# Row scaling of the softmax weights in the latent attention: GpSimd alone, or two blocks each on GpSimd and ScalarE

## Chip, cores and metric

The kernel runs on one core of one Trainium2 chip. The metric is the device time of one execution in microseconds (us), taken as the median of several runs. For the kernel before it is 1179.66 us (three runs, 1179.07 to 1180.35).

The core has five engines that run side by side, each taking its own instructions strictly in order: TensorE (PE in the profile; its weight loads are PEld), VectorE (DVE), ScalarE (ACT), GpSimd (POOL) and SyncE (SP, which here only starts transfers). They wait for each other by semaphores.

## Reference

Two layers of an encoder on 512 tokens of 1024 channels, float32. Each layer normalises its input, projects it by one wide matrix, runs three token mixers side by side, gates and merges them, and adds the projected sum to the stream. The part at stake is the first mixer, the latent attention (MLA), with 8 heads:

```python
def attend(qb):                       # one block of 128 query rows, all heads
    s = jnp.einsum('bqhd,bkhd->bhqk', qb, k).astype(jnp.float32) * scale
    p = jax.nn.softmax(s, axis=-1).astype(v.dtype)
    return jnp.einsum('bhqk,bkhd->bqhd', p, v)
```

So for each head there is a 512 x 512 matrix P = exp(s - rowmax), of which each row is divided by its sum before it is multiplied by V. The other two mixers are a windowed attention with sinks and a differential attention; they have softmaxes of their own that the change does not touch.

## The kernel before, in words

Matrix products are done in a split form: each float32 operand is cut into a high part (a rounded copy, written by ScalarE with `act_copy`, line 81) and a low part (the rest, by VectorE with `sub`, line 84), and `mm3` (lines 86 to 89) adds the three products high x high, high x low and low x high. A projection of 128 columns (`proj_T`) is therefore 24 matmuls into the PSUM tile `ps_dn`. Its weights come through `wunit` (lines 102 to 116): a 512 KB load into `wr` (two buffers), a ScalarE cast to `wh` (three buffers), a VectorE subtraction to `wl` (three buffers). The `wr` buffers are also used by `mod_late` (line 245), which loads the next layer's modulation weights during layer 0 and multiplies them up on VectorE (line 251).

Latent attention (`mla_attention`) goes head by head in a software pipeline (`pipelined`): `first(h+1)` is issued ahead of `second(h)`.

- `first(h)`: for each of four blocks of 128 query rows, scores into `ps_sc` (`mm3`), the negated row maximum on VectorE (line 770), the exponential on ScalarE with the row sums as by-product (line 771), all into one tile `p` of 128 x 4 x 512 (two buffers). Then one VectorE reciprocal of the four columns of sums (line 773), and four scalings of 128 x 512 in place (line 775), one for each block, all on GpSimd.
- `second(h)`: for each of four blocks of keys, the four 128 x 128 pieces of P are transposed by TensorE into `ps_tr` (line 704), split into high and low `pt` (ScalarE line 81, VectorE line 84), and multiplied by V into `ps_av` (lines 711 to 717). Every one of these transposes' groups reads all four row blocks of P.

The order on each engine is not written by hand. The program is a list in program order; a planner takes instructions off it by priority (`tc.high_priority` moves weight units ahead) and by the times that it reckons for each operation and engine, and fixes each engine's queue from that. Projections that come later in the program (the gates of `gates_early`, the queries of the windowed attention) are so placed between the matmuls of the latent attention. Replacing one operation by another can thus change the queues behind it, beyond the operation itself.

Of the kernel before, what the change touches and what calls it, by code (L numbers as in the profile page):

```python
# [14 lines left out]
ALU = mybir.AluOpType  # L15
# [35 lines left out]
def hybrid_kernel(ctx, tc, x, c, w_ada, b_ada, g_pre, g_post, w_in, g_q, w_uq, g_kv, w_ukv,  # L51
# [6 lines left out]
    pe, act, dve, pool, sp = nc.tensor, nc.scalar, nc.vector, nc.gpsimd, nc.sync  # L58
# [4 lines left out]
    def T(tag, shape, dt=F32, bufs=None):  # L63
        count[0] += 1
        return sb.tile(shape, dt, tag=tag, name=f"{tag}_{count[0]}",
                       bufs=bufs or BUFS.get(tag, 1))

    def stat(n):
        return T("st", [P, n], F32, 24)
# [3 lines left out]
    def Q(tag):  # L73
        count[0] += 1
        return ps.tile([P, S], F32, tag=tag, name=f"ps_{tag}_{count[0]}", bufs=PB[tag])

    def f(ap):
        return ap.bitcast(F32)

    def act_copy(out_, in_, scale=1.0):  # L80
        return act.activation(out=out_, in_=in_, func=AF.Copy, scale=scale)  # L81

    def sub(out_, a, b, eng=None):
        return (eng or dve).tensor_tensor(out=out_, in0=a, in1=b, op=ALU.subtract)  # L84

    def mm3(o, ah, al, bh, bl, start, stop):
        pe.matmul(o, ah, bh, start=start, stop=False)  # L87
        pe.matmul(o, ah, bl, start=False, stop=False)  # L88
        pe.matmul(o, al, bh, start=False, stop=stop)  # L89
# [575 lines left out]
    def mla_pair_weights(l, p, tag="pt"):  # L665
        raw = T(tag, [P, S])
        qraw = raw[:, 0:384].rearrange("p (k c) -> p k c", k=2)
        kraw = T(tag, [P, S])[:, 0:256]
        with behind(loads[-2]) if l == 0 else nullcontext():
            sp.dma_start(out=qraw, in_=w_uq[l][:, p * 192:(p + 1) * 192]  # L670
                         .rearrange("(k p) c -> p k c", p=P))
            sp.dma_start(out=kraw, in_=w_ukv[l][:, p * 256:(p + 1) * 256])
        h = T("x5", [P, 2, 640], F32R)
        with behind():
            for k in range(2):
                src = raw[:, k * 192:(k + 1) * 192].rearrange("p (h c) -> p h c", h=2)
                hv = h[:, 0, k * 256:(k + 1) * 256].rearrange("p (h c) -> p h c", h=2)
                lv = h[:, 1, k * 256:(k + 1) * 256].rearrange("p (h c) -> p h c", h=2)
                g = par(l, PR_GQ, k)
                for dst, s0, n in ((0, 0, 96), (96, 80, 16), (112, 64, 16)):  # L680
                    act_copy(hv[:, :, dst:dst + n], src[:, :, s0:s0 + n], g)
                    dve.scalar_tensor_tensor(out=lv[:, :, dst:dst + n], in0=src[:, :, s0:s0 + n],
                                             scalar=g, in1=f(hv[:, :, dst:dst + n]),
                                             op0=ALU.mult, op1=ALU.subtract)
            src = kraw.rearrange("p (h c) -> p h c", h=2)[:, :, 0:64]
            hv = h[:, 0, 512:640].rearrange("p (h c) -> p h c", h=2)
            lv = h[:, 1, 512:640].rearrange("p (h c) -> p h c", h=2)
            g = par(l, PR_GKV)
            act_copy(hv, src, g)
            dve.scalar_tensor_tensor(out=lv, in0=src, scalar=g, in1=f(hv),  # L690
                                     op0=ALU.mult, op1=ALU.subtract)
        return h

    def pipelined(first, second, n):
        prev = first(0)
        for i in range(n):
            nxt = first(i + 1) if i + 1 < n else None
            second(i, prev)
            prev = nxt

    def transposed_block(blocks):
        tr = Q("tr")
        for i, b in enumerate(blocks):
            pe.transpose(tr[:, i * P:(i + 1) * P], b, ident)  # L704
        ph = T("pt", [P, S], F32R)
        pl = T("pt", [P, S], F32R)
        act_copy(ph, tr)
        sub(pl, tr, f(ph))
        return ph, pl

    def av_step(av, v, ph, pl, first, last):
        if not last:
            pe.matmul(av, v, ph, start=first, stop=False)  # L713
            pe.matmul(av[0:64], v[:, 0:64], pl, start=False, stop=False)  # L714
        else:
            pe.matmul(av[0:64], v[:, 0:64], pl, start=False, stop=False)
            pe.matmul(av, v, ph, start=False, stop=True)

    def mla_attention(l, cl, kp, v, wts):
        o_all = []  # L720
        ks, qs = {}, {}

        def weights(p):
            if p < 4 and p not in wts:
                wts[p] = mla_pair_weights(l, p)

        def prep(h):
            if h >= 8:
                return
            p, i = h // 2, h % 2  # L730
            w = wts[p]
            if i == 0:
                ts = [T("op", [P, S], F32R) for _ in range(4)]
                ka = Q("pj")
                mm3(ka, w[:, 0, 512:640], w[:, 1, 512:640], cl[2][:, 0], cl[2][:, 1], True, True)
                for j in range(2):
                    kh, kl = ts[2 * j:2 * j + 2]
                    src = ka[j * 64:(j + 1) * 64]
                    act_copy(kh[0:64], src)
                    sub(kl[0:64], src, f(kh[0:64]))  # L740
                    dve.tensor_copy(out=kh[64:128], in_=f(kp[0:64]))
                    dve.tensor_copy(out=kl[64:128], in_=f(kp[64:128]))
                    ks[h + j] = (kh, kl)
                weights(p + 1)
            qh = T("op", [P, S], F32R)
            ql = T("op", [P, S], F32R)
            qa = Q("pj")
            for k in range(2):
                lo = k * 256 + i * P
                mm3(qa, w[:, 0, lo:lo + P], w[:, 1, lo:lo + P], cl[k][:, 0], cl[k][:, 1],  # L750
                    k == 0, k == 1)
            qf = T("ta", [P, S])
            dve.tensor_tensor(out=qf, in0=qa, in1=rq, op=ALU.mult)
            act_copy(qh, qf)
            sub(ql, qf, f(qh))
            qs[h] = (qh, ql)

        def first(h):
            prep(h + 1)
            if h % 2 == 0:  # L760
                o_all.append(T("o", [P, S]))
            kh, kl = ks[h]
            qh, ql = qs[h]
            pr = T("p", [P, NT, S])
            nm, sm, rr = stat(NT), stat(NT), stat(NT)
            for t in range(NT):
                ts_ = slice(t * P, (t + 1) * P)
                s = Q("sc")
                mm3(s, qh[:, ts_], ql[:, ts_], kh, kl, True, True)
                dve.tensor_reduce(out=nm[:, t:t + 1], in_=s, axis=AX.X, op=ALU.max, negate=True)  # L770
                act.activation(out=pr[:, t], in_=s, func=AF.Exp, bias=nm[:, t:t + 1],  # L771
                               accum_out=sm[:, t:t + 1])
            dve.reciprocal(out=rr, in_=sm)  # L773
            for t in range(NT):
                pool.tensor_scalar(out=pr[:, t], in0=pr[:, t], scalar1=rr[:, t:t + 1],  # L775
                                   scalar2=1.0, op0=ALU.mult, op1=ALU.mult)
            return pr

        def second(h, pr):
            i = h % 2  # L780
            op = o_all[h // 2]
            av = Q("av")
            for kb in range(NT):
                ph, pl = transposed_block([pr[:, t, kb * P:(kb + 1) * P] for t in range(NT)])
                av_step(av, v[kb][:, h], ph, pl, kb == 0, kb == NT - 1)
            ol = T("ta", [P, S])
            act_copy(ol[0:64], av[64:128])
            dve.tensor_tensor(out=op[i * 64:(i + 1) * 64], in0=av[0:64], in1=ol[0:64], op=ALU.add)

        weights(0)  # L790
        prep(0)
        pipelined(first, second, 8)
        return o_all

# [425 lines left out]
```

## Time and profile before

| | |
|---|---|
| median of 3 runs | 1179.66 us (1179.07 to 1180.35) |
| the profiled execution | 1178.78 us, of which the span of the trace is 1176.7 us |
| mean granted TensorE clock | 0.993 |
| PE busy | 1146.0 us (97%) |
| DVE busy | 844.2 us (72%) |
| ACT busy | 631.5 us (54%) |
| POOL busy | 181.3 us (15%) |
| the 64 scalings of line 775, POOL | 52.2 us, 834 ns each on average |

The latent attention lies at about 117 to 260 us (layer 0) and 680 to 829 us (layer 1). "Busy" is the time in which an engine had an instruction in execution; TensorE's matmuls overlap, so two that follow each other without a gap start about 0.23 us apart though each is listed with 0.39 us. A row of a group gives count, busy time, mean duration of one, then the idle time of that engine just before these instructions and what ended it. A row of the timeline gives start, duration, engine, line, operation and tiles, and in brackets the idle time before it.

### The profile page before, as it was taken

What the parts mean: (1) busy time and instruction counts of PE and PEld (TensorE: products, weight loads), DVE (VectorE), ACT (ScalarE), POOL (GpSimd) and SP (SyncE); (2) the same over time, 40 slices, a digit from 0 to 9 for tenths busy, and PEclk for the clock granted to TensorE, in tenths of its full rate; (3) what the DMA queues carried; (4) which work ended last, traced back from release to release, by engine and by line L of the source; (5) the groups of instructions that cost most, each with busy time, mean ns of one, the idle gap of its engine ahead of it and who ended that gap; (6) DMA issues with size and microseconds to landing.
All of it is one profiled execution on the core that took longest, in us unless ns stands there. A gap on an engine that the chain in (4) does not pass through costs nothing.

```text
span 1176.7 us, 15536 instructions
## 1 busy us (share of the span) xinstructions
PE 1146.0 (97%) x5428; PEld 946.0 (80%) x5428; DVE 844.2 (72%) x1754; ACT 631.5 (54%) x1250; POOL 181.3 (15%) x226
## 2 busy tenths in 40 slices
PE   5899999999999999999999999999999999999997
PEld 4768788878887888888888888888888888888886
DVE  7956686898866687876577567688786568786654
ACT  5355464655543457664357456565564346675432
POOL 4310212122210010101211011222121001100120
PEclk9899999999999999999999999999999999999999
DMA  9537532256355433433454432324533333334442
GB/s 340 190 92 217 186 106 76 72 145 186 108 141 164 110 81 87 117 107 126 143 184 135 114 108 75 86 52 123 157 97 92 95 95 96 88 99 115 136 159 92
DMA packets 169522, 146.86 MB, mean 125 GB/s; under 512 B 7679, under 2 KB 146999, under 8 KB 169444
## 3 DMA queue, kind: packets, MB, share of 16 engines
q1 hardware_dynamic: 166148, 140.08, 40.9%
q10 hardware_dynamic: 3168, 5.77, 1.3%
q8 instruction: 43, 0.70, 0.2%
q14 instruction: 35, 0.29, 0.1%
q0 software_dynamic: 128, 0.01, 0.0%
HBM read 135.83 MB, written 14.20 MB: 127 GB/s over the span
## 4 chain that ended last, share of the span: by engine, by line
PE 84%; DVE 6%; DMA 3%; issue 3%; ACT 1%; POOL 1%; SPq 0%; DVEq 0%; POOLq 0%; ACTq 0%
PE ps_dn L87 20%; PE ps_dn L89 20%; PE ps_dn L88 19%; PE ps_tr L704 5%; PE ps_sc L89 2%; PE ps_sc L87 2%; PE ps_sc L88 2%; PE ps_av L714 1%; PE ps_av L713 1%; PE ps_sc L952 1%; PE ps_sc L953 1%; DMA wr<-in_w_in 1%; DVE o L206 1%; PE ps_pj L87 1%; PE ps_pj L88 1%
## 5 line engine op out<-in xcount | busy, mean ns | idle before, releaser
L87 PE MATMUL ps_dn<-hTh,wh 128*128 128x512 f32 x840 | 331.8, 395 | 1.4 <-DVE zz L479 0.8
L89 PE MATMUL ps_dn<-hTh,wl 128*128 128x512 f32 x840 | 330.5, 393 | 0.4 <-DVE wl L84 0.4
L88 PE MATMUL ps_dn<-hTl,wh 128*128 128x512 f32 x840 | 330.1, 393 | 0.0
L84 DVE TENSOR_TENSOR wl<-wr,wh 128x1024 fp32r<-128x1024 f32 x141 | 178.9, 1269 | 98.5 <-ACT wh L81 97.5
L81 ACT ACTIVATE wh<-wr 128x1024 fp32r<-128x1024 f32 x141 | 149.1, 1058 | 162.7 <-PE ps_dn L88 111.2
L87 PEld LDWEIGHTS ps_dn<-hTh,wh 128*128 128x128 f32 x840 | 158.2, 188 | 33.2 <-PE ps_dn L89 1.0
L89 PEld LDWEIGHTS ps_dn<-hTh,wl 128*128 128x128 f32 x840 | 158.0, 188 | 33.3 <-DVE wl L84 0.9
L88 PEld LDWEIGHTS ps_dn<-hTl,wh 128*128 128x128 f32 x840 | 158.1, 188 | 31.7
L84 DVE TENSOR_TENSOR pt<-ps_tr,pt 128x512 fp32r<-128x512 f32 x136 | 92.2, 684 | 30.5 <-ACT pt L81 29.6
L81 ACT ACTIVATE pt<-ps_tr 128x512 fp32r<-128x512 f32 x136 | 78.8, 596 | 64.8 <-PE ps_tr L704 63.6
L775 POOL TENSOR_SCALAR p<-p,st 128x512 f32<-128x512 f32 x64 | 52.2, 834 | 279.3 <-DVE st L773 243.7
L704 PE MATMUL ps_tr<-ident,p 128*128 128x128 f32 x544 | 92.4, 273 | 0.9 <-POOL p L775 0.6
L704 PEld LDWEIGHTS ps_tr<-ident,p 128*128 128x128 f32 x544 | 69.5, 141 | 20.2 <-POOL p L775 1.8
L87 PE MATMUL ps_dn<-u,wh 128*128 128x512 f32 x192 | 75.9, 395 | 0.0
L89 PE MATMUL ps_dn<-u,wl 128*128 128x512 f32 x192 | 75.9, 395 | 0.0
L88 PE MATMUL ps_dn<-u,wh 128*128 128x512 f32 x192 | 75.2, 391 | 0.0
L963 POOL TENSOR_SCALAR ta<-ta,st 128x512 f32<-128x512 f32 x32 | 26.7, 834 | 306.9 <-ACT wh L81 143.1
L894 POOL TENSOR_SCALAR p<-p,st 128x256 f32<-128x256 f32 (+1 forms) x64 | 42.1, 676 | 157.7 <-DVE st L892 130.4
L771 ACT ACTIVATE p<-ps_sc,st 128x512 f32<-128x512 f32 x64 | 43.7, 685 | 28.0 <-DVE st L770 27.7
L770 DVE TENSOR_REDUCE st<-ps_sc 128x1 f32<-128x512 f32 x64 | 43.4, 686 | 21.3 <-PE ps_sc L89 20.8
L886 ACT ACTIVATE p<-p,st 128x256 f32<-128x256 f32 (+1 forms) x64 | 35.7, 558 | 21.9 <-DVE st L884 21.2
L959 ACT ACTIVATE p<-p,st 128x512 f32<-128x512 f32 x32 | 23.1, 723 | 38.8 <-DVE st L957 38.7
(345 smaller groups left out, 2100.5 us busy)
## 6 DMA issues: line engine op xcount, KB each, us to landing
wr<-in_w_in SPq DMA_DIRECT2D x105, 512.0 KB, 3.7
wr<-in_w_ada SPq DMA_DIRECT2D x32, 512.0 KB, 3.6
wr<-in_w_out SPq DMA_DIRECT2D x16, 512.0 KB, 3.6
big<-in_w_ada SPq DMA_DIRECT2D x10, 512.0 KB, 7.6
big<-in_x SPq DMA_DIRECT2D x8, 512.0 KB, 5.3
wr<-in_w_o_mla SPq DMA_DIRECT2D x8, 512.0 KB, 4.0
wr<-in_w_o_swa SPq DMA_DIRECT2D x8, 512.0 KB, 3.4
wr<-in_w_o_diff SPq DMA_DIRECT2D x8, 512.0 KB, 3.7
```

The source lines that it names most:

```text
L81: return act.activation(out=out_, in_=in_, func=AF.Copy, scale=scale)
L84: return (eng or dve).tensor_tensor(out=out_, in0=a, in1=b, op=ALU.subtract)
L87: pe.matmul(o, ah, bh, start=start, stop=False)
L88: pe.matmul(o, ah, bl, start=False, stop=False)
L89: pe.matmul(o, al, bh, start=False, stop=stop)
L704: pe.transpose(tr[:, i * P:(i + 1) * P], b, ident)
L770: dve.tensor_reduce(out=nm[:, t:t + 1], in_=s, axis=AX.X, op=ALU.max, negate=True)
L771: act.activation(out=pr[:, t], in_=s, func=AF.Exp, bias=nm[:, t:t + 1], accum_out=sm[:, t:t + 1])
L775: pool.tensor_scalar(out=pr[:, t], in0=pr[:, t], scalar1=rr[:, t:t + 1], scalar2=1.0, op0=ALU.mult, op1=ALU.mult)
L886: act.activation(out=pr[:, i, :w], in_=pr[:, i, :w], func=AF.Exp, bias=nm[:, i:i + 1], accum_out=sm[:, i:i + 1])
L894: pool.tensor_scalar(out=pr[:, i, :w], in0=pr[:, i, :w], scalar1=rr[:, i:i + 1], scalar2=1.0, op0=ALU.mult, op1=ALU.mult)
L963: pool.tensor_scalar(out=pc[1], in0=pc[1], scalar1=rr[:, 1:2], scalar2=1.0, op0=ALU.mult, op1=ALU.mult)
```

## The change

Of the four row blocks of a head, the even ones (t = 0, 2) are still scaled by GpSimd. The odd ones (t = 1, 3) are scaled by ScalarE: `act_copy` is an activation of the kind Copy whose scale is the column of reciprocals. Input, output and values stay; there are 16 heads in both layers, so 32 of the 64 scalings move.

```diff
             dve.reciprocal(out=rr, in_=sm)
             for t in range(NT):
-                pool.tensor_scalar(out=pr[:, t], in0=pr[:, t], scalar1=rr[:, t:t + 1],
-                                   scalar2=1.0, op0=ALU.mult, op1=ALU.mult)
+                if t % 2 == 0:
+                    pool.tensor_scalar(out=pr[:, t], in0=pr[:, t], scalar1=rr[:, t:t + 1],
+                                       scalar2=1.0, op0=ALU.mult, op1=ALU.mult)
+                else:
+                    act_copy(pr[:, t], pr[:, t], rr[:, t:t + 1])
             return pr
```

## The prediction

> **What bounds the kernel now.** I read the page's totals first, then the busy time of each engine by stage, then what TensorE waits for, and last the order of time at the two places where it waits.
>
> ```profile
> PE 1146.0 (97%) x5428; PEld 946.0 (80%) x5428; DVE 844.2 (72%) x1754; ACT 631.5 (54%) x1250; POOL 181.3 (15%) x226
> ```
>
> TensorE has work in 97% of the span. The table by stage, with stretches cut at the two latent attentions, tells where the other 3% lies:
>
> ```profile
> core 0: us, PE busy (x) PEld busy (x) DVE busy (x) ACT busy (x) POOL busy (x), PEclk, DMA share, GB/s
> 117.00:245.00 128.00, 127.28 (x625) 103.22 (x624) 99.61 (x164) 74.75 (x153) 26.60 (x32) 1.00 0.39 115
> 245.00:260.00 15.00, 12.86 (x59) 10.17 (x59) 13.06 (x32) 7.12 (x16) 1.84 (x4) 0.89 0.63 163
> 260.00:680.00 420.00, 418.99 (x1988) 349.27 (x1987) 299.64 (x653) 226.82 (x444) 51.03 (x64) 1.00 0.44 128
> 680.00:810.00 130.00, 130.00 (x635) 106.54 (x634) 96.26 (x158) 77.46 (x159) 25.61 (x32) 1.00 0.30 84
> 810.00:1150.00 340.00, 340.00 (x1603) 280.97 (x1602) 239.00 (x510) 181.74 (x328) 46.00 (x56) 1.00 0.39 113
> ```
>
> The columns are the length of the stretch, then busy time and count by engine, then the granted TensorE clock. From 117 to 1150 us, 1029.1 of 1033 are busy: 3.9 us of idleness are all that any edit of this stage could hand back, and what follows 1150 and comes before 117 is not touched by it. In layer 1 the attention (680 to 810) shows no idle time at all. The other engines are far from full: ScalarE has 74.75 of 128 us (58%), GpSimd 26.6 (21%).
>
> What TensorE waited for from 117 to 250 us, whole list (total, times, longest):
>
> ```profile
> PE ps_sc L878 <- DVE st L880: 1.1, 1, 1.1
> PE ps_av L713 <- DVE st L884: 0.9, 1, 0.9
> PE ps_tr L704 <- POOL p L775: 0.6, 2, 0.3
> ```
>
> The scalings held TensorE up by name for 0.6 us, twice. They are not the bound. The two larger waits are on VectorE.
>
> **The change, part by part.** *What moves.* 32 of 64 scalings leave GpSimd and come to ScalarE:
>
> ```profile
> L775 POOL TENSOR_SCALAR p<-p,st 128x512 f32<-128x512 f32 x64 | 52.2, 834 | 279.3 <-DVE st L773 243.7 <-PE ps_pj L89 14.1 <-PE ps_dn L88 11.6
> L81 ACT ACTIVATE wh<-wr,prT 128x512 fp32r<-128x512 f32 x2 | 1.4, 714 | 1.1 <-PE ps_dn L88 1.1
> L81 ACT ACTIVATE u<-o 128x512 fp32r<-128x512 f32 x24 | 14.3, 622 | 4.6 <-DVE o L991 3.1 <-DVE o L796 1.5
> ```
>
> GpSimd loses 32 x 0.834 = 26.7 us of its 52.2. For ScalarE the trace has the same form, a Copy of 128 x 512 from SBUF to SBUF with a column as scale, twice: 0.714 us; without a column it is 0.622. I take 0.714, so 32 x 0.714 = 22.8 us, 11.4 for each layer. ScalarE goes from 74.75 to 86.2 of 128 us in layer 0 (67%) and from 77.5 to 88.9 of 130 in layer 1 (68%). That lies beside TensorE's work and costs nothing while the 41 us of idle time that are left in each layer's attention stand where they are needed.
>
> *What it earns at the first head.* Each head's four scalings go one after another behind one reciprocal. Only for the first head of layer 0 does TensorE stand at them:
>
> ```profile
> 129.00 1.05 ACT L81 ACTIVATE wh<-wr 128x1024 fp32r<-128x1024 f32 x1
> 129.13 0.18 DVE L773 RECIPROCAL st<-st 128x4 f32<-128x4 f32 x1
> 129.41 3.74 POOL L775 TENSOR_SCALAR p<-p,st 128x512 f32<-128x512 f32 x4 [54.19 <-DVE st L773]
> 129.95 0.58 ACT L492 ACTIVATE tf<-ps_dn 128x512 f32<-128x512 f32 x1
> 131.34 0.27 PE L704 MATMUL ps_tr<-ident,p 128*128 128x128 f32 x1
> 132.10 0.69 ACT L771 ACTIVATE p<-ps_sc,st 128x512 f32<-128x512 f32 x1 [1.57 <-DVE st L770]
> 132.54 1.21 PE L704 MATMUL ps_tr<-ident,p 128*128 128x128 f32 x6 [0.34 <-POOL p L775]
> 133.51 0.48 PE L88 MATMUL ps_dn<-hTl,wh 128*128 128x512 f32 x1
> 243.88 0.60 PE L704 MATMUL ps_tr<-ident,p 128*128 128x128 f32 x4
> ```
>
> Eight transposes fill TensorE from 131.34 to 133.51, 2.17 us. Four in a row without a wait take 0.60 us (the row of 243.88), the first 0.27, so about 0.11 to 0.13 for each further one: eight are worth some 1.1 us, and 1.1 us are lost (the 0.6 named are part of it, the rest stands inside rows that count as busy). With the change GpSimd's two blocks end near 129.41 + 2 x 0.935 = 131.3, and ScalarE's, placed behind the cast that ends at 130.05, near 130.05 + 2 x 0.69 = 131.4. Then nothing is left to wait for. If the tanh of 129.95 goes first, they end at 132.0 and half is lost. The term is -0.5 to -1.1; I take -1.0, nearer the first, since ScalarE has nothing due between 130.5 and 132.1. What ended last then is the exponentials' wait for the row maxima.
>
> *What it earns at the other 15 heads.* The chain from reciprocal to the last scaled block shortens from 3.26 us (52.2 / 16) to about 1.5, and TensorE does not notice, as it has projections to do until the transposes' turn. 0.
>
> *The wait that is added.* ScalarE now waits for the reciprocal. Behind it in the queue stand the next head's exponentials, the `pt` copies, the tanh of the gates with their stores (ScalarE starts those transfers itself; nobody reads them until layers of work later) and, what matters, the casts of weights:
>
> ```profile
> L81 ACT ACTIVATE wh<-wr 128x1024 fp32r<-128x1024 f32 x141 | 149.1, 1058 | 162.7 <-PE ps_dn L88 111.2 <-issue 20.5 <-DMA wr<-in_w_in 18.9
> ```
>
> Most of the idle time before a cast, 111.2 us, is ended by TensorE's last matmul on an old `wh` buffer: the cast is made as soon as a buffer is free, two units ahead of use. One unit of 24 matmuls at 0.23 us is 5.4 us; less cast and subtraction (about 1.06 and 1.25 us) some 3 us of cover are left, against 2 x 0.714 = 1.4 for a pair of copies. Cost 0 in steady state; 1.4 us where the cover is gone, which is below.
>
> *What it does at the joint.* The one real hole of the middle is where the last head of layer 0 meets the windowed attention (first rows in order of time, then a table of 2 us stretches with the columns of the one above):
>
> ```profile
> 241.76 1.06 ACT L81 ACTIVATE wh<-wr 128x1024 fp32r<-128x1024 f32 x1 [0.34 <-DMA wr<-in_w_in]
> 243.40 1.23 DVE L84 TENSOR_TENSOR wl<-wr,wh 128x1024 fp32r<-128x1024 f32 x1
> 244.65 0.37 SPq L112 DMA_DIRECT2D wr<-in_w_in  x1
> 248.64 1.06 ACT L81 ACTIVATE wh<-wr 128x1024 fp32r<-128x1024 f32 x1 [2.97 <-DMA wr<-in_w_in]
> 251.48 0.78 PE L87 MATMUL ps_dn<-hTh,wh 128*128 128x512 f32 x1
> 246.00:248.00 2.00, 0.87 (x5) 0.59 (x4) 1.97 (x6) 0.00 (x0) 0.00 (x0) 1.00 1.05 257
> 248.00:250.00 2.00, 1.13 (x5) 0.66 (x4) 1.97 (x7) 1.33 (x2) 0.00 (x0) 0.83 0.82 239
> 250.00:252.00 2.00, 2.00 (x8) 1.56 (x7) 1.97 (x5) 1.95 (x7) 0.00 (x0) 0.50 0.04 13
> 252.00:254.00 2.00, 2.00 (x9) 1.59 (x7) 1.94 (x4) 1.14 (x4) 0.00 (x0) 0.82 0.76 178
> ```
>
> Here one `wr` buffer feeds the projections: load, cast, subtraction, next load, 6.9 us from cast to cast, while TensorE uses a unit up in 5.4. VectorE is full (1.97 of 2). TensorE idles 1.13 + 0.87 = 2.0 us, and the granted clock falls after it: 0.17 + 0.50 + 0.18 of 2 us each, 1.7 us. The hole's price is 3.7 us. GpSimd's last four scalings lie in the run-up and slow VectorE:
>
> ```profile
> 227.06 1.29 DVE L84 TENSOR_TENSOR u<-o,u 128x512 fp32r<-128x512 f32 x2
> 236.23 4.41 POOL L775 TENSOR_SCALAR p<-p,st 128x512 f32<-128x512 f32 x4 [16.27 <-DVE st L773]
> 237.88 1.09 DVE L84 TENSOR_TENSOR u<-o,u 128x512 fp32r<-128x512 f32 x1
> 238.90 1.18 DVE L251 SCALAR_TENSOR_TENSOR u<-wr,cact,u 128x512 f32<-128x512 f32 x1
> L251 DVE SCALAR_TENSOR_TENSOR u<-wr,cact,u x14: 710/751/1175, 105.7 to 240.8; 128x512 f32<-128x512 f32 x14
> ```
>
> Beside GpSimd one subtraction takes 1.09 instead of 0.65 us and one accumulation 1.18 instead of 0.75: 0.87 in all. Half as much GpSimd work should spare about half, 0.4 us, which the full VectorE passes on to the subtraction at 243.40 (its cast ended at 242.82, so up to 0.58 can be passed on). Bounds: 0 to -0.87; I take -0.4.
>
> *The sum.* -1.0 - 0.4 = -1.4 us. On the profiled execution's own time of 1178.78 (a span of 1176.7 and 2.1 around it) that is 1177.4. The median of the runs shown is 0.88 above that execution, so 1179.66 - 1.4 = 1178.3 us. That is 0.12%, and a measurement of this kernel tells about 0.2% (2.4 us) from no change: the forecast is no visible change.
>
> *What the sum can't hold.* The planner reckons with other engines and times from 129 us on and may order all that follows anew. TensorE's 5428 instructions stay the same, so a new order can only open or close holes. Closing all of them gives the 3.9 us of idleness, 1.7 of clock and 1.1 at the first head: -6.7 at most. A hole that opens is priced by the joint's, +3.7.
>
> **The rivals.** *The joint's hole closes (faster).* If the scaled last head, 2 us earlier, lets the planner put its transposes and products where TensorE now stands idle, the 3.7 us go: -1.0 - 3.7 = -4.7, 1175.0 us. For it: `p` is ready only at 240.64 there, and TensorE has ready work missing from 246. Against: the hole ends with the weights of 248.64, whose load waits for VectorE and not for P.
>
> *The copies stand before a cast that is due (slower).* At the joint the cast at 241.76 begins 0.3 us after its load landed. If the pair of the last head, or exponentials pushed back by it, stand in front, each round is up to 1.4 us later, the idle time goes from 2.0 to 3.4 and the clock's part stays or grows; if such a place arises at another spot, it costs another 3.7. With the first head's gain: -1.0 + 3.7 = +2.7, 1182.4 us. It decides once a cast starts later than its landing by more than the cover of 3 us in steady state, or by anything at the joint. For it: ScalarE's queue is strictly in order and goes from 58 to 67%. Against: the last head's reciprocal is done by 236.23, where GpSimd starts, so its copies could end 3 us ahead of that cast.
>
> The Trainium skill, page "TensorE: Matmul & The Clock Gate", section "The HAM clock gate", says that the clock falls to half only after a whole idle window of about 3.4 us; by that rule a hole like the joint's would cost its 2.0 us alone and this rival would end at 1180.7, within no change. The trace disagrees here: no idle piece was longer than 1.13 us, and the clock was 0.50 from 250 to 252 us, so I price it by the trace.
>
> *The change does not shorten the chain.* If ScalarE reaches the copies late each time, P is complete no earlier than now and the first head's gain is gone; -0.4 remains, 1179.3 us. This too is no visible change.
>
> **How the numbers follow.** No visible change (the sum, or the chain not shortened): 0.47. The joint closes or another order closes as much: 0.25. A new hole: 0.28; rather more than the closing since there is little idle time left to close, and one engine gets more work. The predicted time is 1178.3; its own range, with the terms at their bounds, is 1177.5 to 1179.7. The range over the cases is 1174.5 to 1183.5: it takes in the one closed and the one new hole with their small terms and leaves out two new holes (1186) and the closing of everything (1173).
>
> **What would show it.** Line 775 has 32 GpSimd instructions, of a mean below 0.834 us, and line 81 has 32 new `p<-p` copies near 0.71. ScalarE's busy time is some 23 us more, GpSimd's some 27 less. From 131 us on the eight transposes take 1.1 us with no wait for `p`. From 680 to 810 TensorE has no idle time. VectorE's instructions at the joint show no 1.1 us ones. I am wrong if TensorE shows idle pieces of a microsecond that are not there now, with clock values below 1.00 behind them, or if 246 to 254 us is filled at full clock.

## The result: 17 us slower, and the profile after

The changed kernel takes 1196.43 us (median of four runs, 1195.18 to 1197.24), the kernel before, run beside it, 1179.37 (1178.67 to 1180.35): a ratio of 1.0139, with a 95% interval of 1.0127 to 1.0151. The forecast of 1178.3 and its range up to 1183.5 are both missed. The profiled execution took 1195.18 us, with a span of 1193.4.

The totals first (engine, busy time, share of the span, instructions), from the page of the kernel after:

```profile
PE 1154.9 (97%) x5428; PEld 950.3 (80%) x5428; DVE 839.6 (70%) x1754; ACT 650.5 (55%) x1282; POOL 152.8 (13%) x194
```

The moved work looks as forecast: ScalarE 19.0 us more than before, GpSimd 28.5 less, TensorE still 97%. From the groups of instructions, shapes kept apart, of the kernel after, first ScalarE's copies, then GpSimd's half:

```profile
L81 ACT ACTIVATE p<-p,st 128x512 f32<-128x512 f32 x32 | 21.4, 719 | 2.5 <-DVE st L773 2.4
L776 POOL TENSOR_SCALAR p<-p,st 128x512 f32<-128x512 f32 x32 | 25.5, 809 | 301.8 <-DVE st L773 288.2 <-PE ps_dn L89 13.7
```

None of this is the loss. The table by stage of the kernel after finds it (length of the stretch, busy time and count by engine, granted TensorE clock):

```profile
core 0: us, PE busy (x) PEld busy (x) DVE busy (x) ACT busy (x) POOL busy (x), PEclk, DMA share, GB/s
117.00:200.00 83.00, 82.72 (x398) 67.03 (x397) 60.03 (x102) 54.18 (x112) 8.23 (x10) 1.00 0.42 129
200.00:245.00 45.00, 39.78 (x178) 30.55 (x177) 36.49 (x62) 27.16 (x54) 5.80 (x6) 0.89 0.37 103
245.00:330.00 85.00, 79.40 (x386) 64.68 (x385) 61.88 (x173) 44.35 (x100) 13.35 (x24) 0.92 0.38 109
330.00:680.00 350.00, 349.35 (x1637) 291.07 (x1636) 241.30 (x500) 185.30 (x354) 37.07 (x44) 1.00 0.44 125
680.00:825.00 145.00, 145.00 (x702) 118.57 (x701) 104.37 (x171) 94.52 (x189) 11.50 (x16) 1.00 0.32 90
```

and the two stretches that differ, of the kernel before, with the same columns:

```profile
200.00:245.00 45.00, 45.00 (x229) 36.53 (x228) 38.59 (x62) 26.02 (x52) 10.49 (x12) 1.00 0.31 91
245.00:330.00 85.00, 82.86 (x416) 68.71 (x416) 71.41 (x194) 47.36 (x108) 17.27 (x27) 0.98 0.50 141
```

All of it lies between 200 and 330 us, in the second half of layer 0's latent attention and the windowed attention behind it. TensorE idles 5.2 + 5.6 = 10.8 us there (before: 2.1), and the clock takes 0.11 x 45 + 0.08 x 85 = 11.8 us (before: 0.02 x 85 = 1.7). That is 18.8 us more; less the 0.8 us that the first head earns (below) it makes 18.0, beside 16.7 between the two spans. The sum is a little high, since clock lost while TensorE stands idle is counted twice in it. Layer 1, with the same edit, is as full as it was.

What TensorE waited for from 200 to 330 us, kernel after (total, times, longest; all rows but the smallest):

```profile
PE ps_av L714 <- DVE pt L84: 4.2, 4, 2.4
PE ps_sc L87 <- ACT p L771: 1.4, 1, 1.4
PE ps_av L713 <- DVE o L913: 1.3, 1, 1.3
PE ps_av L713 <- DVE o L791: 1.1, 1, 1.1
PE ps_pj L826 <- DVE ta L753: 1.1, 1, 1.1
PE ps_dn L87 <- DVE ashf L261: 1.1, 1, 1.1
```

No row, the smallest included, names a scaled `p` of line 81 or 776, and none a cast `wh` of line 81. TensorE waits for the attention's own short chain: transposed P split by VectorE (`pt`), exponentials, a finished head. These chains are there before too; something used to fill their waits. The hole at 215 us, the same table in steps of 5 us:

```profile
215.00:220.00 5.00, 2.62 (x12) 1.24 (x10) 4.25 (x8) 4.64 (x11) 0.00 (x0) 1.00 0.17 29
220.00:225.00 5.00, 3.51 (x12) 2.31 (x13) 4.97 (x9) 2.49 (x5) 1.77 (x2) 0.66 0.56 176
225.00:230.00 5.00, 3.65 (x12) 2.53 (x11) 4.88 (x9) 3.11 (x7) 0.00 (x0) 0.50 0.25 64
230.00:235.00 5.00, 5.00 (x23) 4.02 (x22) 4.81 (x9) 3.15 (x7) 0.00 (x0) 0.81 0.16 59
```

And the same steps with the projection matmuls into `ps_dn` alone (length, TensorE's busy time and count, clock, DMA share, GB/s), first after, then before:

```profile
220.00:225.00 5.00, 0.00 (x0) 0.66 0.56 176
225.00:230.00 5.00, 0.00 (x0) 0.50 0.25 64
```

```profile
220.00:225.00 5.00, 4.76 (x20) 1.00 0.64 202
225.00:230.00 5.00, 2.28 (x10) 1.00 0.04 11
```

Before, 30 projection matmuls stand in these 10 us, after none. TensorE's order of time in the kernel after shows the edges of that stretch and what it holds:

```profile
215.38 0.40 PE L89 MATMUL ps_dn<-hTh,wl 128*128 128x512 f32 x1
216.90 0.65 PE L826 MATMUL ps_pj<-ident,tf 128*128 128x128 f32 x4 [1.12 <-DVE ta L753]
...
219.44 0.47 PE L713 MATMUL ps_av<-pt,big 128*128 128x512 f32 x1 [1.15 <-DVE o L791]
220.55 0.45 PE L714 MATMUL ps_av<-pt,big 128*64 128x512 f32 x1 [0.64 <-DVE pt L84]
...
227.53 0.79 PE L87 MATMUL ps_sc<-op,op 128*128 128x512 f32 x1 [1.35 <-ACT p L771]
...
232.52 0.48 PE L87 MATMUL ps_dn<-hTh,wh 128*128 128x512 f32 x1
```

For 17 us, from 215.38 to 232.52, no projection stands between the attention's matmuls, and five times TensorE waits 0.64 to 1.35 us for the VectorE or ScalarE step in front of the next one. That is an order of the queue, not a length of an operation. So I read TensorE's queues out of the programs and counted, for each P tile of layer 0, how many projection matmuls are queued ahead of its first and of its last transpose (some rows; "backwards" and the columns right of it are kernels 5, 6, 9 and 12 of the experiments below):

```
            before    after     backwards  one on ACT  projections later  all on ACT
head 2      304-322   305-320   313-331    304-321     305-320            314-343
head 3      331-357   339-359   353-376    328-362     331-355            343-370
head 4      361-388   378-394   394-412    366-387     363-388            388-394
head 5      388-418   416-418   418-418    389-418     388-418            413-418
head 6      442-473   418-442   418-438    442-472     418-466            418-439
head 7      477-494   466-490   457-478    484-494     476-494            461-490
window 0    522-538   517-517   522-522    522-538     522-538            520-520
window 1    576-597   543-565   563-586    576-597     576-597            556-577
```

Up to head 5 the changed queue spends its projections early: 416 of them stand ahead of head 5's first transpose instead of 388, only two lie between that head's transposes instead of 30, and head 6 begins at 418 with none in between. From head 6 on it is the other way round, and the first two windowed blocks come up to 33 matmuls sooner.

### The profile page after: what moved, and what is told of

Read it like the earlier page. It is cut to its first block, busy times and chain, and to the rows that moved or that the text cites. A ratio compares the mean times of both kernels' runs of the same rounds, so it can differ in the third digit from the quotient of the medians.

```text
span 1193.4 us, 15521 instructions
## 1 busy us (share of the span) xinstructions
PE 1154.9 (97%) x5428; PEld 950.3 (80%) x5428; DVE 839.6 (70%) x1754; ACT 650.5 (55%) x1282; POOL 152.8 (13%) x194
## 4 chain that ended last, share of the span: by engine, by line
PE 81%; DVE 8%; DMA 5%; issue 3%; ACT 2%; POOL 1%; SPq 0%; DVEq 0%; POOLq 0%; ACTq 0%
PE ps_dn L87 19%; PE ps_dn L88 19%; PE ps_dn L89 19%; PE ps_tr L704 4%; DMA wr<-in_w_ada 2%; PE ps_sc L89 2%; PE ps_sc L87 2%; PE ps_sc L88 2%; DVE wl L84 1%; PE ps_av L714 1%; PE ps_sc L955 1%; PE ps_sc L956 1%; DVE o L206 1%; DMA wr<-in_w_in 1%; PE ps_av L713 1%
## 5 line engine op out<-in xcount | busy, mean ns | idle before, releaser
L704 PEld LDWEIGHTS ps_tr<-ident,p 128*128 128x128 f32 x544 | 69.8, 141 | 18.5 <-issue 0.6
L776 POOL TENSOR_SCALAR p<-p,st 128x512 f32<-128x512 f32 x32 | 25.5, 809 | 301.8 <-DVE st L773 288.2
L897 POOL TENSOR_SCALAR p<-p,st 128x256 f32<-128x256 f32 (+1 forms) x64 | 39.6, 638 | 174.7 <-DVE st L895 111.6
```

What stands on the lines that cost most here:

```text
L897: pool.tensor_scalar(out=pr[:, i, :w], in0=pr[:, i, :w], scalar1=rr[:, i:i + 1], scalar2=1.0, op0=ALU.mult, op1=ALU.mult)
```

## The experiments

Theory A: the planner, which fixes each engine's queue from the operations it is given, wrote another TensorE queue, and its order alone makes the holes. Theory B: the loss comes from the operations themselves, the copies on ScalarE and the weaker use of GpSimd. "Held" below means that an engine's instructions are chained in a recorded order by dependencies that order the issue and carry no semaphore.

**1 and 2. Order and operations crossed.** The first kernel has the change with every engine's queue held to that of before (the 32 copies go where they may); the second leaves all 64 scalings on GpSimd and holds every other queue to that of the changed kernel.

```diff
         hybrid_kernel(tc, *args)
+        pin_order(tc, ORDER)      # 1: queues of before under the changed code
+                                  # 2: queues of after under the code of before
```

> The change (two blocks on GpSimd, two on ScalarE), but every engine's queue is held to that of the kernel before; only the 32 copies are put in where the planner finds them ready. Theory order (the 17 us come from the new queues, not from the copies): back to 1177 to 1181 us, the first head's wait for p gone (about -1). Theory ScalarE (the copies in ScalarE's strict queue hold up the pt copies, exponentials and casts behind them): still 1190 to 1198 us, with holes at 215 to 230 us.

> The reverse: all 64 scalings on GpSimd as before, but every other instruction stands in the queues of the changed kernel. Theory order: 1193 to 1199 us, with holes at 215 to 230 and 255 to 260 us. Theory ScalarE: 1178 to 1182 us, since ScalarE is relieved of the 22.8 us.

The first took 1176.9 us (ten runs), a ratio of 0.9982 (0.9971 to 0.9993) to the kernel before; the second 1196.73, 1.0148 (1.0131 to 1.0165). New operations in the old order are a little faster than before; old operations in the new order have the whole loss. The stage tables, first of the change in old queues, then of the old code in new queues:

```profile
200.00:245.00 45.00, 45.00 (x227) 36.57 (x226) 38.59 (x63) 30.18 (x60) 5.45 (x6) 1.00 0.30 93
245.00:330.00 85.00, 82.36 (x425) 68.56 (x424) 71.39 (x196) 47.63 (x110) 16.88 (x28) 1.00 0.50 145
```

```profile
200.00:245.00 45.00, 41.00 (x195) 31.81 (x194) 37.00 (x60) 24.92 (x51) 10.29 (x12) 0.96 0.34 101
245.00:330.00 85.00, 77.88 (x379) 63.49 (x378) 62.94 (x175) 44.13 (x101) 13.70 (x25) 0.92 0.38 112
```

**3. The other two blocks.** Blocks 0 and 2 on ScalarE.

```diff
-                if t % 2 == 0:
+                if t % 2 == 1:
```

> The change with the parts swapped: blocks 0 and 2 on ScalarE, 1 and 3 on GpSimd, queues as the planner makes them. The load of each engine is that of the changed kernel. Theory ScalarE: the same 1196 us within 2. Theory order: the planner sees other times, so another set of queues and a time that need not be 1196; anything from 1175 to 1200, and a difference of over 4 us from the changed kernel speaks for it.

1194.32 us, 1.0134 (1.0116 to 1.0151). The planner gave TensorE the queue of the changed kernel (the counts of all eight heads are the same), so both theories fit: it tells nothing between them.

**4. TensorE's queue alone.** The change, with only TensorE held to its queue of before; the other engines are the planner's.

> The change, with TensorE's queue alone held to that of the kernel before; ScalarE, VectorE, GpSimd and SyncE are queued by the planner around it. Theory order, in the form that TensorE spent its projections too early: 1177 to 1182 us, as with all queues held. If it is VectorE's or ScalarE's queue that matters: 1185 to 1198 us. Theory ScalarE: 1190 to 1198 us.

1176.92 us (ten runs), 0.9983 (0.9974 to 0.9992). Holding this one queue is enough. The others then come out nearly as before by themselves: compared place by place in the traces, leaving out the scalings of `p`, VectorE's order differs from that of before in 41 of 1754 places, in the changed kernel in 419. TensorE's old queue together with the other engines' new ones was not run, so their share by themselves is not shown.

**5. The old operations in another order.** The kernel before, with GpSimd scaling the four blocks from the last to the first; nothing moves to another engine.

```diff
-            for t in range(NT):
+            for t in reversed(range(NT)):
                 pool.tensor_scalar(out=pr[:, t], in0=pr[:, t], scalar1=rr[:, t:t + 1],
```

> The kernel before with one edit: the four GpSimd scalings of a head are written in the order t = 3, 2, 1, 0. Engines, operations and their number are unchanged; the planner makes new queues, in which TensorE has 418 projection matmuls of layer 0 in front of head 6's first transpose (before: 442, changed kernel: 418) and 563 in front of the windowed attention's second block (before 576, changed 543). Theory lead (the time goes with how far the attention is queued ahead of the projections): slower than before by 5 to 12 us, with the hole at 215 to 230 us. Theory that the copies on ScalarE are needed for the loss: 1178 to 1182 us.

1194.94 us, 1.0128 (1.0113 to 1.0143): more than expected, and nearly the loss of the change without a single operation on ScalarE. The column "backwards" shows the same shift (head 4 at 394, head 5 at 418), and its stages show holes in the same two stretches; layer 1 idles another 2.7 us (680 to 825 us):

```profile
200.00:245.00 45.00, 38.76 (x188) 30.34 (x186) 38.05 (x61) 24.37 (x50) 9.96 (x12) 0.96 0.31 91
245.00:330.00 85.00, 80.36 (x395) 65.62 (x394) 64.30 (x171) 43.36 (x97) 12.26 (x22) 0.96 0.42 121
```

**6. A quarter of the load.** Only block 3 on ScalarE (`if t < 3` for GpSimd), queues left to the planner.

> Three blocks on GpSimd, only the last (t = 3) on ScalarE; queues as the planner makes them, and they come out nearly as before: 442 projection matmuls in front of head 6's first transpose, 576 in front of the windowed attention's second block. Theory lead: 1176 to 1180 us. Theory that any move to ScalarE costs in proportion: a quarter of the scalings moved instead of half, about half of the loss, 1186 to 1190 us.

1178.93 us (ten runs), 0.9995 (0.9985 to 1.0004): no change. With half as many copies theory B would have lost about half; here the queue stayed nearly that of before (column "one on ACT"), and so did the time.

**7 and 8. Which part of the order.** The change with the first transposes of heads 6 and 7 held back behind as many projection matmuls as before (442 and 477); and the change with the windowed blocks' first transposes held back to the old counts.

```diff
+        hold_back(tc, [(transpose, projection matmul), ...])   # two pairs; eight pairs
```

> The changed kernel plus two constraints for the planner: in layer 0 the first transposes of heads 6 and 7 are queued behind as many projection matmuls as in the kernel before (442 and 477; 418 and 466 without it). All else is left to the planner; the windowed attention then starts at 546 projection matmuls instead of 517. Theory lead: the holes of 215 to 230 us are gone and most of those behind them, 1177 to 1184 us. If TensorE's queue matters elsewhere (heads 0 to 5): 1190 to 1197 us.

> The changed kernel plus constraints on the eight blocks of layer 0's windowed attention only: their first transposes are queued behind as many projection matmuls as in the kernel before; heads 6 and 7 stay early. Theory lead, holes being independent: the hole of 215 to 230 us stays (about 9 us), those of 255 to 305 us go (about 8 us): 1185 to 1190 us. If the holes are one thing that is only moved about: 1192 to 1198 us.

The first took 1189.2 us, 1.0076 (1.0061 to 1.0091), the second 1189.47, 1.0083 (1.0068 to 1.0098). The first misses its expectation. In steps of 5 us, it closes the hole at 255 us, but that of 215 to 230 stays:

```profile
225.00:230.00 5.00, 3.57 (x10) 2.49 (x11) 4.86 (x10) 2.88 (x7) 0.04 (x1) 0.50 0.26 85
255.00:260.00 5.00, 5.00 (x26) 4.17 (x25) 4.82 (x10) 1.71 (x4) 0.00 (x0) 1.00 0.37 98
```

So heads 6 and 7 coming early are not what opens the first hole. The second kernel meets its time, but not by closing the places where the holes begin:

```profile
220.00:225.00 5.00, 4.23 (x13) 2.77 (x13) 5.00 (x9) 2.77 (x6) 1.77 (x2) 0.66 0.50 162
225.00:230.00 5.00, 3.65 (x21) 2.49 (x19) 4.85 (x10) 3.60 (x8) 0.00 (x0) 1.00 0.24 60
255.00:260.00 5.00, 0.77 (x3) 0.34 (x2) 4.35 (x7) 1.68 (x5) 0.00 (x0) 0.87 0.29 70
```

The hole at 255 us is deeper than in the changed kernel (2.60 busy there), and that of 215 to 230 us still idles 3.9 us instead of 5.2, at a better clock. Holding back what comes early repairs single holes. Both start behind heads 3 to 5, whose transposes have more projections ahead of them than before; that is what the next kernel tests.

**9. The start of it.** The change with six constraints: the projection matmul that follows the first and the last transpose of heads 3, 4 and 5 in the queue of before is queued behind that transpose here too. Everything else is the planner's.

```diff
+        queue_behind(tc, [(projection matmul, transpose), ...])   # six pairs
```

> The changed kernel plus six constraints on TensorE's queue in layer 0, all before the first hole: the projection matmul that follows the first (and the last) transpose of heads 3, 4 and 5 in the kernel before is queued behind that transpose here too. That takes back what the changed kernel does early: 339, 378 and 416 projection matmuls in front of the three heads' first transposes instead of 331, 361 and 388. Everything else is left to the planner; head 6 still starts at 418 instead of 442, the windowed attention comes out at 522, 576, 598 as before. Theory of the two faces (projections spent too early up to 215 us, attention without projections after it): the hole of 215 to 230 us closes and 1176 to 1184 us. If the loss sits in heads 6 and 7 or in the windowed attention: 1188 to 1196 us.

1178.68 us (ten runs), 0.9990 (0.9981 to 0.9999). Six edges give back all 17 us, and the later counts mend themselves (column "projections later"), all but head 6's first, which stays at 418. The two stages, then the projection matmuls alone:

```profile
200.00:245.00 45.00, 45.00 (x226) 36.74 (x225) 38.24 (x62) 30.04 (x59) 5.37 (x6) 1.00 0.31 91
245.00:330.00 85.00, 82.59 (x415) 68.74 (x414) 70.92 (x187) 48.28 (x109) 14.72 (x24) 0.96 0.50 144
```

```profile
220.00:225.00 5.00, 2.52 (x11) 1.00 0.27 75
225.00:230.00 5.00, 3.19 (x15) 1.00 0.46 138
```

**10 and 12. All four blocks on ScalarE.** In the old queues (10), and as the planner has it (12).

> All four scalings of a head on ScalarE (45 us more than before instead of 23), every other instruction in the queues of the kernel before. Theory queues: ScalarE has room, 1176 to 1181 us, some of the first head's gain given back since four copies follow each other. Theory ScalarE's load: 1185 us or more.

> All four scalings on ScalarE, queues as the planner makes them: 418 projection matmuls in front of head 6's first transpose and 413 in front of head 5's (before 442 and 388), 556 in front of the windowed attention's second block. Same engines and operations as the run with the old queues. Theory queues: 1186 to 1196 us, 8 to 18 above that run. Theory load: both the same within 3 us.

1178.08 us, 0.9986 (0.9977 to 0.9996) in the old queues; 1195.08 us, 1.0131 (1.0115 to 1.0148) in the planner's. The same operations, 17.0 us apart. With twice the copies of the change ScalarE still costs TensorE little when the order is the old one: the one wait that the copies lengthen stands behind the first head's four (1.34 us for an exponential, 0.29 in kernel 1). From 117 to 245 us ScalarE is then busy for 73% (the busy column alone):

```profile
117.00:245.00 128.00, 93.59 (x186) 1.00 0.38 116
```

**11. A better queue, tried.** Kernel 4 with eight matmuls of one projection put off to the joint at 245 us, where TensorE waits.

> The change with TensorE's queue of the kernel before, in which eight matmuls of one projection are put off: four to just ahead of the windowed scores and four to just ahead of the products that TensorE waits for at 246 to 249 us. The other engines are queued by the planner. If that hole is only a lack of projection matmuls in that place: 1174 to 1176.5 us, a little below the same kernel without the shift (1176.9). If the put-off projection's own readers come late for it: 1177 to 1181 us.

1183.52 us, 1.0034 (1.0020 to 1.0048): outside every expectation. What TensorE waits for from 200 to 340 us is now a split of transposed P (1.8 us, at 245 us) and, longest, the windowed attention's own scaling (at 287 us):

```profile
PE ps_tr L704 <- POOL p L897: 4.0, 1, 4.0
```

The hole moved and grew; the attempt failed. The planner also wrote the other engines' queues anew around the moved matmuls, so whether these or the put-off matmuls make the long wait is not shown.

Put together, as ratios to the kernel before:

| scalings on ScalarE | TensorE in the old queue | TensorE in a new queue |
|---|---|---|
| none | 1 | 1.0148 (kernel 2), 1.0128 (kernel 5) |
| 32 of 64 | 0.9982, 0.9983 (kernels 1, 4) | 1.0139 (the change), 1.0134 (kernel 3) |
| all 64 | 0.9986 (kernel 10) | 1.0131 (kernel 12) |

Down a column the time moves by 0.2%, along each row by 1.3 to 1.6%. The new queues of kernels 5 and 12 are not that of the change, but they spend projections early in the same way. Theory B falls. Kernels 1 and 4 are the fastest: 0.18% under the kernel before, 1.6% under the changed one; kernels 10 and 9 lie between them and the kernel before.

## Why the prediction was wrong, step by step

**The step that failed: "What the sum can't hold".** It named the cause (the planner may order all that follows anew) and then priced it by one hole of the joint's size, +3.7 us, with a chance of 0.28 for any new hole. What came was a queue in which several holes follow from one shift: the six rows of waits shown are 10.2 us of idle time, with 11.8 us of clock around them. Between kernel 1 and the changed kernel, which have the same operations, the order is worth 18.5 us by their ratios. The bound "a new order can only open or close holes" fits what came; taking one hole for the far end did not. The price of a whole order that is worse had no row in the trace of before. One ingredient was there: from 220 to 230 us 30 projection matmuls stand between the attention's matmuls, and TensorE is full. What 17 us without them cost, 5.2 us of idle time and 5.2 of clock, shows only in the trace after. The far end should have been several holes, and the chance of "slower" higher. The prediction's own sign of being wrong did come: idle pieces of a microsecond that were not there, with clock values below 1.00 behind them.

**The slower rival** had the right sign, and not the mechanism of the loss. It expected copies in front of a due cast. That happens at the first head, at a price of 0.6 us (below); between 200 and 330 us, where the loss lies, TensorE waits for no cast and no copy.

**ScalarE and GpSimd: right.** 0.719 us for a copy (forecast 0.714), 0.809 for a GpSimd block (forecast: below 0.834). ScalarE's total grew by 19.0, not by some 23: consecutive copies overlap, a pair takes 1.34 us and all sixteen pairs 21.4. Where the other 2.4 us went is not shown.

**First head of layer 0: right, by two errors that cancel.** The kernel after, in order of time:

```profile
129.29 1.34 ACT L81 ACTIVATE p<-p,st 128x512 f32<-128x512 f32 x2 [0.24 <-DVE st L773]
129.35 1.38 POOL L776 TENSOR_SCALAR p<-p,st 128x512 f32<-128x512 f32 x2 [54.56 <-DVE st L773]
131.26 1.04 PE L704 MATMUL ps_tr<-ident,p 128*128 128x128 f32 x8
132.05 0.47 PE L88 MATMUL ps_dn<-hTl,wh 128*128 128x512 f32 x1
134.43 0.50 PE L87 MATMUL ps_sc<-op,op 128*128 128x512 f32 x1 [0.28 <-ACT p L771]
```

Both pairs are done by 130.73, and eight transposes hold up the next matmul for 0.79 us instead of 2.17. That gains 1.4 us, not 1.0: eight without a wait are worth 0.8, where I had reckoned 1.1. But 0.6 of it goes again at once. The next scores (last row) wait for an exponential, which they did not before; the prediction named the exponentials' wait ("What ended last then") and put no cost on it. It comes from the copies: they stand in front of a cast, which starts at 130.53 instead of 129.00; VectorE's subtraction waits for that cast (2.36 us), and the row maximum queued behind it starts at 132.87 instead of 131.37, the exponential at 133.59 instead of 132.10. From the first transpose to the last matmul of these scores it is 131.26 to 135.00 = 3.74 us, before 131.34 to 135.89 = 4.55: 0.8 us of net gain, inside the forecast's 0.5 to 1.1. I had put the copies behind that cast.

In kernels 1 and 4 the same stretch takes 3.73 and 3.75 us; in kernel 10, where four copies follow each other, 4.99, so that nothing is left of the gain. In the profiles of kernels 1 and 4 TensorE also waits 0.3 and 0.5 us for an exponential just ahead of these transposes, before any scaling. The kernel before has no such wait, and its cause is open.

**The other 15 heads, and layer 1: right.** With the order held, no wait for `p` is left and layer 1 has no idle time; it has none with the new order either.

**The joint: the term was right, and the clock came on top.** The accumulations of line 251 are faster, as said: their longest was 1175 ns, and in kernel 1

```profile
L251 DVE SCALAR_TENSOR_TENSOR u<-wr,cact,u x14: 712/748/752, 106.8 to 240.6; 128x512 f32<-128x512 f32 x14
```

the longest is 752. The subtraction beside GpSimd still takes 1.09, so only one of the two slow instructions is gone. From the last head's reciprocal to the subtraction at the joint it is 235.89 to 243.40 = 7.51 us before, 236.13 to 243.20 = 7.07 in kernel 1 and 235.55 to 242.62 = 7.07 in kernel 4: 0.44 less, where 0.4 was forecast. TensorE's first wait at the joint, 1.13 us before, is shorter too; in kernel 1:

```profile
246.79 0.38 PE L881 MATMUL ps_sc<-op,op 128*128 128x256 f32 x1 [0.57 <-DVE st L883]
```

What the sum did not have is the clock there: the stretch from 245 to 260 us, table by stage of kernel 1, has

```profile
245.00:260.00 15.00, 12.36 (x68) 10.05 (x68) 12.44 (x32) 7.39 (x16) 1.41 (x4) 1.00 0.56 149
```

against 12.86 at 0.89 before: 1.7 us of clock back, 0.5 of idle time more (a new wait of 1.21 us stands at 259 us). In kernel 4 it is 12.68 at 1.00, in kernel 10 12.69 at 0.96. First head -0.8 and joint -1.2 make -2.0; by their ratios kernels 1 and 4 measure -2.1 and -2.0 us, with intervals from -3.4 to -0.8. So close a fit is luck, since the open wait ahead of the first head is left out. That the joint's clock is a lasting effect of the edit is not shown: it is read from one profile of each kernel. The mean clocks of all runs point the same way (median 0.992 for the kernel before, 0.9935 and 0.994 for kernels 1 and 4).

**The sum's own range.** With the terms at their bounds, -1.97 and -0.5, it is 1177.7 to 1179.2 us, not 1177.5 to 1179.7. Nothing hangs on it.

**Open.** What in the planner's reckoning tips it to the other queue. Turning a loop round tips it (kernel 5), so does moving two or four blocks, moving one does not (kernel 6). No run here looks into its costs.

## What to carry to other kernels

Where a planner orders the engines' queues, a swap of one operation is two changes, the operation and the order, and here the second weighed some nine times the first; compare the queues before believing a sum of durations, and hold them fixed to time the operation alone. Where one engine is 97% busy because long independent work fills the waits of a short chain, count how much of that filler is queued ahead of each step of the chain: spending it early costs nothing then and the idle time and the clock later. Here six ordering constraints at the place where the filler was spent mended what constraints on the heads and blocks behind it did not. Where an edit shortens one wait, measure up to a point well behind it: at the first head 0.6 of the 1.4 us went again within the next matmuls.

## What was not expected of the hardware

Short waits can cost as much by the clock as by themselves. In the kernel after, pieces of 0.6 to 1.35 us between 215 and 230 us go with a granted clock of 0.66, 0.50 and 0.81 over 15 us, 5.2 us lost beside 5.2 idle. In kernel 8 the same hole idles 3.9 us, and after one slice at 0.66 the clock is back at 1.00. Before, 1.13 + 0.87 us of idle time in 4 us brought the clock to 0.50; in kernel 1, 0.76 + 0.68 in the same 4 us left it at 1.00:

```profile
246.00:248.00 2.00, 1.24 (x6) 0.59 (x4) 1.94 (x8) 0.00 (x0) 0.00 (x0) 1.00 1.07 279
248.00:250.00 2.00, 1.32 (x7) 0.98 (x8) 2.00 (x8) 1.81 (x3) 0.00 (x0) 1.00 0.61 220
```

Yet the amount of idle time does not decide it either. In kernel 5 TensorE idles 2.29 of 5 us, and the clock stays at 1.00 in this stretch and the next:

```profile
225.00:230.00 5.00, 2.71 (x16) 1.79 (x15) 4.94 (x9) 3.47 (x7) 2.20 (x4) 1.00 0.40 105
230.00:235.00 5.00, 5.00 (x26) 4.08 (x25) 4.81 (x9) 2.81 (x7) 0.00 (x0) 1.00 0.37 94
```

In kernel 6 1.03 + 0.59 us in the 4 us from 244 to 248 brought it to 0.50. So neither the longest piece nor the sum over a few microseconds foretells the clock in these traces. What does is open, and no threshold was measured.
